# Attention blocks with two steps from scores to transposes, gate rows loaded per block, and the sixth token's first half moved ahead

## The chip, the cores and the metric

The kernel runs on one core of one Trainium2 chip. The metric is the device time of one execution in microseconds (us). The engines are PE (matrix multiplication, with PEld for its weight loads), DVE (vector), ACT (activations), POOL (GpSimd) and SP, which here only issues DMAs. Each engine runs its own instructions in order and waits on semaphores for the others.

## What is computed

One decoder block of 1024 positions of width 1024 in float32. After a norm and one projection, half of the width goes through a gated MLP (part A), half through forgetting attention with eight heads of 64 (part B). Both halves are normed, joined and projected; then follows a gated feed-forward network.

```python
n = rmsnorm(x);  proj = n @ w_in
a_out = spatial_gating(gelu(proj_u), gelu(proj_v), ...)          # part A
log_f = log_sigmoid(f_logit + b_f);  c = cumsum(log_f)           # part B
logits = (q_blk @ k_blk.T) * scale + c[q0:q1, None] - c[None, :q1]
p = softmax(where(mask, logits, -inf));  b_out = p @ v_blk
merged = concat(rmsnorm(a_out), rmsnorm(b_out));  mix = merged @ w_out
h = x + rmsnorm(mix);  out = h + rmsnorm(swiglu(rmsnorm(h)))
```

## The kernel before

Positions are cut into 8 token tiles of 128. Matrix products in float32 are made of three products of halves (`mm3`: high by high, high by low, low by high), so each operand is split on ACT (`L116`, high) and DVE (`L117`, low).

Attention takes the heads in four pairs. A pair has 8 units; a unit is one head `h` and one `m` of 0, 3, 1 or 2, and has two blocks, `i = 2m` and `2m + 1`: 128 queries against the `(i + 1) * 128` keys up to them. So there are 64 blocks, 16 in a pair, in the order 0, 1, 6, 7, 0, 1, 6, 7, 2, 3, 4, 5, 2, 3, 4, 5. Each block goes through four steps:
- `prep`: POOL adds the column `csq` to the gate row `cb` and writes the sum to the row tile `sm` (`L484`), then sets its masked part (`L486`). There are three `sm` tiles. `cb` holds the 1024 gate values of one head on all partitions. `cb_load` fetches it for the two heads of a pair.
- `scores`: PE makes the scores in one or two banks (`L502`) from the query piece `qu` and the keys; DVE adds the row and takes the least value (`L504`), ACT makes the exponential in `sm` (`L507`).
- `probs`: PE transposes the exponentials (`pt`, `L518`), ACT and DVE split them.
- `values` and `finish`, once per unit: PE multiplies with the values (`o`, `L547` to `L550`), ACT copies the result (`osb`, `L552`), PE transposes it back (`ot`, `L559`), ACT and DVE add its halves to `bt`, and for a pair of heads SP stores it to `bo_d`.

The loop over `n` runs the steps staggered: `prep` of block `n + 3`, `scores` of `n + 2`, `probs` of `n + 1`, and at every second `n` the values of a finished unit or the finish of the one before. Query pieces are loaded per unit in four DMAs (`qu_load`, `L471`). In the first three pairs `pump` fills the gaps with the projection matmuls of the next pair (`qk`), paced by the cost of the blocks. In the last pair the stages load the output weights (`load_wo`: `woraw`, eight loads of 512 KB over three stage buffers, split by ACT, DVE and POOL), and from step `SA` on `pump` fills with the output projection (`mx`) of tokens 0 and 1. `merge_a`, `merge_norm` and `merge_b` bring the two halves of a token to PE in transposed form (`tp_ma`, `tp_mb`); `mix_part` projects the four chunks `KA` of part A and the four `KB` of part B; `mix_tail` norms the result and adds x. `ORDER` lists the tokens: 0, 1, 6, 7, 2, 4, 3, 5. The text calls token 6, third in that list, the sixth token.

The order within an engine is not the program's: a scheduler places each instruction by its own estimate of when it can start, with the program's order as the priority. A DMA on SP also waits until the eighth DMA before it has landed, since eight semaphores take turns.

Of the kernel before, what the change touches and what calls it, by code (L numbers as in the profile page):

```python
# [7 lines left out]
F32 = mybir.dt.float32  # L8
# [23 lines left out]
LATE = 4  # L32
ORDER = [0, 1, 6, 7, 2, 4, 3, 5]
WB = 5
SMB = 3
QB = 2
QUB = 2
BTB = 3
# [2 lines left out]
FC = 2.0  # L41
WOS = (0, 1, 2, 3, 6, 7, 8, 9)
SA = 6
SB = 14
SLOPE = 90
LEAD = 10

# [2 lines left out]
def hybrid_block(ctx: ExitStack, tc: tile.TileContext, io: dict, out: bass.AP):  # L50
# [345 lines left out]

    at_cm = pool("att")
    at = at_cm.__enter__()
    qp, ks_, qus, cbs = {}, {}, {}, {}

    def qk_tile(tag, name, bufs):
        return at.tile([P, S], F32R, tag=tag, name=name, bufs=bufs)

    def cb_tile(name, dt=F32):
        return at.tile([P, S], dt, tag="cb", name=name, bufs=2)

    def osb_tile(name):
        return at.tile([P, 2 * P], F32, tag="osb", name=name, bufs=OSB)
# [9 lines left out]
    rrow = at.tile([P, S], F32, tag="rrow", name="rrow")  # L418
    nc.sync.dma_start(out=rrow.rearrange("p (t n) -> p t n", n=P),
                      in_=c_d[NH * NT:, :].rearrange("t n -> (t n)").partition_broadcast(P))  # L420
    cb0 = [cb_tile(f"cb_0_{h}") for h in range(2)]
    osb0 = osb_tile("osb_first")

    def cb_load(p):
        for h in range(2):
            c = cb_tile(f"cb_{p}_{h}") if p else cb0[h]
            g0 = (2 * p + h) * NT
            nc.sync.dma_start(out=c.rearrange("p (t n) -> p t n", n=P),
                              in_=c_d[g0:g0 + NT, :].rearrange("t n -> (t n)").partition_broadcast(P))
            cbs[2 * p + h] = c  # L430
# [42 lines left out]
    class Block:  # L473

        def __init__(self, unit, i):
            self.u, self.i = unit, i
            self.n = (i + 1) * P
            self.nm = f"{unit.hh}_{i}"

        def prep(self):  # L480

            i, n, hh = self.i, self.n, self.u.hh
            self.sm = sm = at.tile([P, S], F32, tag="sm", name=f"sm_{self.nm}", bufs=SMB)
            nc.gpsimd.tensor_scalar(out=sm[:, :n], in0=cbs[hh][:, :n], scalar1=csq[:, hh * NT + i:hh * NT + i + 1],  # L484
                                    scalar2=1.0, op0=ALU.add, op1=ALU.mult)
            nc.gpsimd.affine_select(out=sm[:, i * P:n], in_=sm[:, i * P:n], pattern=[[-1, P]], base=0,  # L486
                                    channel_multiplier=1, compare_op=ALU.is_ge, fill=BIG)
# [209 lines left out]
    qk_load(0, 1)  # L697
    for _ in qk_steps(0):
        pass
    cb_load(0)  # L700
    def qk_stream():
        for p in range(1, NPAIR):
            yield from qk_steps(p)
# [3 lines left out]
    def pump(upto):  # L707
        nonlocal done
        while done < upto:
            next(fill, None)  # L710
            done += 1
# [7 lines left out]
        x = (sum(cost[:m]) + part * cost[m]) / whole  # L719
        return min((NPAIR - 1) * QS, int(x * SLOPE + min(LEAD, 100 * x)))  # L720

    for n in range(-3, NB + 1):
        m = n + 2
        p, s = divmod(m, PB)
        if n + 3 < NB:
            if (n + 3) % PB == 0 and n + 3 > 0:
                cb_load((n + 3) // PB)
                pump((n + 3) // PB * QS)
            if (n + 3) % 2 == 0:
                qu_load(units[(n + 3) // 2])  # L730
            blocks[n + 3].prep()
        if 0 <= m < NB:
            if m == last:
                q0_cm.__exit__(None, None, None)
# [5 lines left out]
                nc.sync.dma_start(out=gb, in_=io["out_norm_b_gain"].partition_broadcast(P))  # L740
            blocks[m].scores()
        if last <= m:
            s = m - last
# [15 lines left out]
            if s == 9:  # L759
                for t in range(2):  # L760
                    nc.sync.dma_start(out=ab2[t], in_=bo_d[t * P:(t + 1) * P, :])
            if s in (11, 12):
                merge_norm(s - 11, ab2[s - 11], gb, junk)
            if s in (SB - 1, SB):
                merge_b(s - SB + 1, ab2[s - SB + 1])
            if s == SB:
                for _ in fill:
                    pass
                fill, done = mix_chain([(0, 0, KB, None), (0, 1, KB, None), (1, 0, KB, None)]), 0
            if s == 15:  # L770
                gains = [cb_tile(nm) for nm in ("gpm_att", "gpf_att")]
                load_gains(gains)
            if SA <= s < SB:
                pump((s - SA + 1) * 12 // (SB - SA))
            if s >= SB:
                pump((s - SB + 1) * 12 // (19 - SB))
        elif m >= 0:
            pump(pace(m, 0.5))
        if 0 <= n + 1 < NB:
            blocks[n + 1].probs()  # L780
        if 0 <= m < last:
            pump(pace(m, 1.0))
        if n >= 0 and n % 2 == 1:
            units[n // 2].values()
        if n >= 2 and n % 2 == 0:
            units[n // 2 - 1].finish(bts)
    for _ in fill:
        pass
    x_load(0)
# [36 lines left out]
    ab = {}  # L826

    def merge_start(t):
        a = ab[t] = flat(vs_tile(ORDER.index(t) % 2, f"ab_{t}"))
        rows = slice(t * P, (t + 1) * P)  # L830
        nc.sync.dma_start(out=a[:, :AW], in_=an_d[rows, :])
        nc.sync.dma_start(out=a[:, AW:], in_=bo_d[rows, :])
# [105 lines left out]
    order = ORDER  # L938
    merge_start(order[2])
    merge_start(order[3])  # L940
    for i, t in enumerate(order):
        if i == 7:
            raw_early(0, 1, 2)
        if i >= 2:
            for step, _ in enumerate(mix_chain([(t, 0, KALL, "mm"), (t, 1, KALL, "S")])):
                if i == 7 and step == 4:
                    pair_first(1)
                if i == 7 and step == 11:
                    norm2_first(3)
        if i in (3, 4, 6):  # L950
            j = {3: 0, 4: 1, 6: 2}[i]
            norm2_first(j)
            norm2_second(j)
        if i + 2 < NT:
            t2 = order[i + 2]
            merge_norm(t2, ab[t2][:, AW:], gb, junk)
        if i >= 2:
            mix_tail(t, gains, i == 7)
        if i + 2 < NT:
            x_load(t2)  # L960
            k = 2 + 2 * (i % 2)
            merged[t2] = (vs_tile(k, f"mh_{t2}"), vs_tile(k + 1, f"ml_{t2}"))
            merge_a(t2, ab[t2])
            merge_b(t2, ab[t2][:, AW:])
        if i + 4 < NT:
            merge_start(order[i + 4])
# [349 lines left out]
```

## Time and profile before

| | us |
|---|---|
| median of 3 runs (1131.88 to 1133.18) | 1132.99 |
| the profiled execution, whole | 1133.7 |
| its span, first to last instruction | 1132.0 |
| PE busy | 1095.6 |
| DVE busy | 719.4 |
| ACT busy | 527.9 |
| POOL busy | 162.6 |

The span is what the trace covers, and 1.7 us of the profiled execution lie outside of it. A busy PE is not PE at its peak, since matmuls overlap and their ends are modelled; what counts is how far apart their starts are. In a list of waits, "PE s L502 <- DVE st L504" means that PE stood before an instruction of line 502 and that the last event that it needed came from DVE's line 504. The granted clock is the share of PE's full 2.4 GHz.

### The profile page before, as it was taken

What the parts mean: (1) busy time and instruction counts of PE and PEld (TensorE: products, weight loads), DVE (VectorE), ACT (ScalarE), POOL (GpSimd) and SP (SyncE); (2) the same over time, 40 slices, a digit from 0 to 9 for tenths busy, and PEclk for the clock granted to TensorE, in tenths of its full rate; (3) what the DMA queues carried; (4) which work ended last, traced back from release to release, by engine and by line L of the source; (5) the groups of instructions that cost most, each with busy time, mean ns of one, the idle gap of its engine ahead of it and who ended that gap; (6) DMA issues with size and microseconds to landing.
All of it is one profiled execution on the core that took longest, in us unless ns stands there. A gap on an engine that the chain in (4) does not pass through costs nothing.

```text
span 1132.0 us, 15484 instructions
## 1 busy us (share of the span) xinstructions
PE 1095.6 (97%) x5353; PEld 910.2 (80%) x5353; DVE 719.4 (64%) x1225; ACT 527.9 (47%) x1017; POOL 162.6 (14%) x235
## 2 busy tenths in 40 slices
PE   6999999999999989999999999999999999999997
PEld 6988777888877768777888888888888888888885
DVE  6576325676668646789775667566756364644666
ACT  5444324666668534464433333333333345454552
POOL 3043113443337321000000000000000000000001
PEclk9999999999999999999999999999999999999999
DMA  7621013333255354457765564556455489766665
GB/s 263 213 93 33 34 74 105 86 88 103 75 156 166 118 191 139 158 182 227 260 225 186 189 217 163 204 177 237 154 191 185 145 287 321 224 191 195 192 201 169
DMA packets 87825, 192.99 MB, mean 170 GB/s; under 512 B 10236, under 2 KB 28740, under 8 KB 85060
## 3 DMA queue, kind: packets, MB, share of 16 engines
q1 hardware_dynamic: 87748, 192.01, 52.1%
q8 instruction: 42, 0.69, 0.3%
q14 instruction: 35, 0.29, 0.1%
HBM read 134.00 MB, written 49.58 MB: 162 GB/s over the span
## 4 chain that ended last, share of the span: by engine, by line
PE 81%; DVE 6%; DMA 4%; ACT 3%; issue 3%; POOL 2%; SPq 1%; POOLq 0%; DVEq 0%; ACTq 0%
PE guA L120 7%; PE guA L121 7%; PE guA L122 7%; PE guC L121 3%; PE guC L122 3%; PE guC L120 3%; PE dA L121 3%; PE dA L122 3%; PE dA L120 3%; PE dC L122 3%; PE dC L120 3%; PE dC L121 3%; PE qk L122 2%; PE qk L121 2%; PE qk L120 2%
## 5 line engine op out<-in xcount | busy, mean ns | idle before, releaser
L104 POOL TENSOR_TENSOR st<-st,mhalf 128x1 f32<-128x1 f32 x17 | 12.1, 715 | 663.4 <-DVE st L102 663.4
L117 DVE TENSOR_TENSOR dal<-dar,dah 128x512 fp32r<-128x512 f32 x77 | 53.2, 692 | 82.6 <-ACT dah L116 82.6
L116 ACT CAST dah<-dar 128x512 fp32r<-128x512 f32 x77 | 47.9, 622 | 97.9 <-PE dA L121 52.1
L117 DVE TENSOR_TENSOR ptl<-pt,pth 128x512 fp32r<-128x512 f32 (+2 forms) x96 | 51.6, 554 | 27.8 <-ACT pth L116 27.1
L121 PE MATMUL dA<-dwl,dah 128*128 128x512 f32 x176 | 68.7, 390 | 0.2 <-DVE dwl L117 0.2
L120 PE MATMUL dA<-dwh,dah 128*128 128x512 f32 x176 | 68.5, 389 | 0.0
L122 PE MATMUL dA<-dwh,dal 128*128 128x512 f32 x176 | 68.5, 389 | 0.0
L484 POOL TENSOR_SCALAR sm<-cb,csq 128x128 f32<-128x128 f32 (+3 forms) x64 | 50.8, 794 | 98.2 <-PE pt L518 75.1
L507 ACT ACTIVATE sm<-sm,st 128x128 f32<-128x128 f32 (+3 forms) x64 | 49.9, 780 | 17.4 <-DVE st L504 16.6
L116 ACT CAST pth<-pt 128x512 fp32r<-128x512 f32 (+2 forms) x96 | 43.6, 476 | 26.2 <-PE pt L518 25.8
L117 DVE TENSOR_TENSOR dwl<-dwr,dwh 128x512 fp32r<-128x512 f32 x77 | 52.7, 685 | 2.3 <-ACT dwh L116 2.3
L117 DVE TENSOR_TENSOR fbc_0l<-ts,fbc_0h 128x1024 fp32r<-128x1024 f32 x22 | 26.9, 1224 | 42.1 <-ACT fbc_0h L116 42.1
L502 PE MATMUL s<-k,qu 128*128 128x384 f32 (+4 forms) x192 | 51.1, 368 | 2.6 <-DVE st L504 2.4
L120 PE MATMUL qk<-nth,qkw 128*128 128x512 f32 x128 | 53.4, 418 | 0.0
L120 PE MATMUL mx<-woh,mh 128*128 128x512 f32 x128 | 52.2, 408 | 1.2 <-ACT mh L116 1.1
L122 PE MATMUL mx<-woh,ml 128*128 128x512 f32 x128 | 50.9, 400 | 1.2 <-DVE ml L117 1.2
L120 PE MATMUL dC<-dwh,dah 128*128 128x512 f32 x132 | 51.3, 389 | 0.0
L121 PE MATMUL dC<-dwl,dah 128*128 128x512 f32 x132 | 51.3, 389 | 0.0
L122 PE MATMUL dC<-dwh,dal 128*128 128x512 f32 x132 | 51.3, 389 | 0.0
L121 PE MATMUL mx<-wol,mh 128*128 128x512 f32 x128 | 51.2, 400 | 0.0
L121 PE MATMUL qk<-ntl,qkw 128*128 128x512 f32 x128 | 50.7, 396 | 0.0
L122 PE MATMUL qk<-nth,qkw 128*128 128x512 f32 x128 | 50.5, 395 | 0.1
(749 smaller groups left out, 3243.4 us busy)
## 6 DMA issues: line engine op xcount, KB each, us to landing
graw<-in_w_gu SPq DMA_DIRECT2D x21, 1024.0 KB, 5.4
wj<-in_w_ffn_out SPq DMA_DIRECT2D x22, 512.0 KB, 4.1
aj<-ff_d SPq DMA_DIRECT2D x22, 512.0 KB, 4.3
dar<-as_d SPq DMA_DIRECT2D x44, 256.0 KB, 3.8
dwr<-ws_d SPq DMA_DIRECT2D x44, 256.0 KB, 3.9
dwr<-in_w_ffn_out SPq DMA_DIRECT2D x33, 256.0 KB, 4.2
dar<-ff_d SPq DMA_DIRECT2D x33, 256.0 KB, 4.3
ff_d<-g SPq DMA_DIRECT2D x22, 256.0 KB, 5.4
```

The source lines that it names most:

```text
L104: nc.gpsimd.tensor_tensor(out=r, in0=m, in1=mhalf, op=ALU.pow)
L116: nc.scalar.copy(out=hi, in_=src)
L117: (lo_eng or nc.vector).tensor_tensor(out=lo, in0=src, in1=hi.bitcast(F32), op=ALU.subtract)
L120: nc.tensor.matmul(o, ah, bh, start=first, stop=False, **kw)
L121: nc.tensor.matmul(o, ah, bl, start=False, stop=False, **kw)
L122: nc.tensor.matmul(o, al, bh, start=False, stop=last, **kw)
L484: nc.gpsimd.tensor_scalar(out=sm[:, :n], in0=cbs[hh][:, :n], scalar1=csq[:, hh * NT + i:hh * NT + i + 1], scalar2=1.0, op0=ALU.add, op1=AL ...
L502: nc.tensor.matmul(o[:, :w], qu[:, hl, ts], ks_[hh][:, ks], start=hl == 0, stop=hl == 1)
L507: nc.scalar.activation(sm[:, :n], sm[:, :n], AF.Exp, bias=m, scale=-1.0, accum_out=rsum[:, self.i, hh:hh + 1])
```

## The change

The row tiles `sm` become five, and `cb` goes. Each block now has a step `load` that fetches its own part of the gate row by a broadcast DMA right into `sm`; `prep` adds to it in place. The loop is staggered by one step more between scores and transposes: `load` of `n + 5`, `prep` of `n + 4`, `scores` of `n + 3`, `probs` of `n + 1`. `finish` comes before `values` at odd `n`, two iterations behind the values of its unit. The steps that prepare tokens 0 and 1 move back by two (`SB` and the constants 9 to 12). Token 6 gets its part A loaded into a row tile and transposed within the loop, its `KA` product directly behind token 1's tail, and the third turn of the later loop is written out there.

```diff
-SMB = 3
+SMB = 5
...
-SB = 14
+SB = 16
...
+        def load(self):
+
+            self.sm = sm_tile(f"sm_{self.nm}")
+            g0 = self.u.hh * NT
+            nc.sync.dma_start(out=self.sm[:, :self.n].rearrange("p (t n) -> p t n", n=P),
+                              in_=c_d[g0:g0 + self.i + 1, :].rearrange("t n -> (t n)").partition_broadcast(P))
...
-            nc.gpsimd.tensor_scalar(out=sm[:, :n], in0=cbs[hh][:, :n], scalar1=csq[:, hh * NT + i:hh * NT + i + 1],
+            nc.gpsimd.tensor_scalar(out=sm[:, :n], in0=sm[:, :n], scalar1=csq[:, hh * NT + i:hh * NT + i + 1],
...
-    for n in range(-3, NB + 1):
-        m = n + 2
...
+    blocks[0].load()
+    for n in range(-4, NB + 2):
+        m = n + 3
+        s = m - last
+        if n + 5 < NB:
+            blocks[n + 5].load()
+        if n + 4 < NB:
+            if (n + 4) % PB == 0:
+                pump((n + 4) // PB * QS)
+            if n % 2 == 0:
+                qu_load(units[n // 2 + 2])
+            blocks[n + 4].prep()
...
+            if s == 16:
+                t2 = ORDER[2]
+                a = sm_tile(f"a_{t2}")[:, :AW]
+                nc.sync.dma_start(out=a, in_=an_d[t2 * P:(t2 + 1) * P, :])
+                merged[t2] = [qk_tile(f"q{x}", f"m{x}_{t2}", 2).rearrange("p (k t) -> p k t", t=P) for x in "hl"]
+                merge_a(t2, a)
...
-                pump((s - SB + 1) * 12 // (19 - SB))
+                pump((s - SB + 1) * 12 // (21 - SB))
...
-        if n >= 0 and n % 2 == 1:
-            units[n // 2].values()
-        if n >= 2 and n % 2 == 0:
-            units[n // 2 - 1].finish(bts)
+        if n % 2 == 1:
+            if n >= 3:
+                units[n // 2 - 1].finish(bts)
+            if 0 < n < NB:
+                units[n // 2].values()
...
+    t = ORDER[2]
+    merge_start(t, (1,))
+    merge_start(ORDER[3])
+    merge_b_norm(2)
+    merge(2)
+    for _ in mix_chain([(t, 0, KA, "mm"), (t, 1, KA, "S")]):
+        pass
+    merge_b_norm(3)
+    merge(3)
+    for _ in mix_chain([(t, 0, KB, None), (t, 1, KB, None)]):
+        pass
```

What this does to the order of the instructions shows at three places. The first is ACT in the last head pair, from the exponential of block 6 of head 6 to the first copy of that block's transposes (`sm_6_6` is head 6, block 6; `pth` the high half of its transposes). Before:

```order
L507 ACTIVATE sm_6_6_3867,rsum_66<-sm_6_6_3867,st1_148_3920 128x896
L116 CAST mh_0_3839<-tp_ma0_0_3931 128x512
L116 CAST pth_6_0_0_3888<-pt_6_1_0_3938 128x2x128
L566 COPY bt_2_2_3752<-ot_5_2_3943 128x2x64
L116 CAST woh3_3972<-woraw3_3970 128x512
L586 CAST woh3_3972<-woraw3_3970 128x512
L116 CAST mh_1_3841<-tp_ma1_0_3978 128x512
L116 CAST pth_6_3_0_3990<-pt_6_6_0_3985 128x4x128
```

The same place on ACT after:

```order
L504 ACTIVATE sm_6_6_3809,rsum_66<-sm_6_6_3809,st1_148_3931 128x896
L549 COPY osb_5_2_3974<-o_5_2_3961 128x256
L116 CAST woh2_3936<-woraw2_3934 128x512
L583 CAST woh2_3936<-woraw2_3934 128x512
L504 ACTIVATE sm_6_7_3880,rsum_66<-sm_6_7_3880,st1_150_3995 128x1024
L116 CAST mh_1_3845<-tp_ma1_0_4006 128x512
L116 CAST pth_6_0_0_3951<-pt_6_1_0_4013 128x2x128
L116 CAST pth_6_3_0_4035<-pt_6_6_0_4030 128x4x128
```

The exponential of the next block, `sm_6_7`, now stands between the two.

The second place is SP's queue in the last pair, around the query pieces of head 7's unit 3 (`qu_7_3`). Before:

```order
L581 DMA woraw3_3970<-in_w_out 128x1024
L581 DMA woraw4_4097<-in_w_out 128x1024
L471 DMA qu_7_3_4040<-qh_3_3007 64x256 x2
L471 DMA qu_7_3_4040<-ql_3_3008 64x256
L570 DMA bo_d_69<-bt_2_2_3752 128x2x128
```

SP at the same place after:

```order
L578 DMA woraw3_3998<-in_w_out 128x1024
L475 DMA sm_7_6_4018<-c_d_70 128x896
L462 DMA qu_7_3_4062<-qh_3_3018 64x256
L475 DMA sm_7_7_4060<-c_d_70 128x1024
L462 DMA qu_7_3_4062<-qh_3_3018 64x256
L462 DMA qu_7_3_4062<-ql_3_3019 64x256
L567 DMA bo_d_69<-bt_2_2_3866 128x2x128
```

The row loads of blocks 6 and 7 of head 7 now stand among the query pieces, each waiting for PE's transposes of the block five places before.

The third place is PE where token 1 ends (`mx_1_1`) and token 6 begins. Before:

```order
L120 MATMUL mx_1_1_4642<-woh7_4239,mh_1_3841 128x512
L121 MATMUL mx_1_1_4642<-wol7_4240,mh_1_3841 128x512
L122 MATMUL mx_1_1_4642<-woh7_4239,ml_1_1_3843 128x512
L129 MATMUL tp_ma6_0_4739<-ident_63,ab_6_4720 128x128 x4
L120 MATMUL mx_6_0_4786<-woh0_3830,mh_6_4737 128x512
L121 MATMUL mx_6_0_4786<-wol0_3831,mh_6_4737 128x512
```

PE at the same place after:

```order
L120 MATMUL mx_1_1_4701<-woh7_4261,mh_1_3845 128x512
L121 MATMUL mx_1_1_4701<-wol7_4262,mh_1_3845 128x512
L122 MATMUL mx_1_1_4701<-woh7_4261,ml_1_1_3847 128x512
L120 MATMUL mx_6_0_4773<-woh0_3834,mh_6_4564 128x512
L121 MATMUL mx_6_0_4773<-wol0_3835,mh_6_4564 128x512
```

The transposes `tp_ma6` have gone ahead into the loop, and token 6's product follows token 1's at once; it is followed by `tp_mb6` as before.

## Rows read from the trace of the kernel before

**Rows 1.** The page: busy time and share of the span, by engine.
```profile
PE 1095.6 (97%) x5353; PEld 910.2 (80%) x5353; DVE 719.4 (64%) x1225; ACT 527.9 (47%) x1017; POOL 162.6 (14%) x235
```
**Rows 2.** Windows: stretch, length, busy by engine; last the clock, DMA share, GB/s.
```profile
187.00:331.00 144.00, 141.73 (x865) 121.41 (x866) 97.48 (x259) 91.79 (x236) 57.30 (x100) 1.00 0.33 86
331.00:345.00 14.00, 11.69 (x70) 9.69 (x69) 13.12 (x33) 12.23 (x30) 6.16 (x9) 0.88 0.72 236
345.00:384.00 39.00, 33.57 (x212) 27.09 (x212) 28.21 (x74) 28.25 (x71) 25.79 (x36) 1.00 0.55 168
384.00:403.30 19.30, 19.30 (x108) 16.21 (x107) 10.71 (x27) 8.97 (x23) 3.19 (x4) 1.00 0.37 124
403.30:407.30 4.00, 1.94 (x10) 1.18 (x9) 2.42 (x5) 1.16 (x3) 0.55 (x1) 1.00 0.35 127
407.30:411.30 4.00, 4.00 (x11) 3.14 (x12) 2.12 (x3) 2.48 (x6) 0.55 (x1) 0.57 0.57 181
```
**Rows 3.** Waits of PE, 331 to 403 us: us in total, times, longest.
```profile
PE s L502 <- DVE st L504: 2.0, 4, 1.1
PE ot L559 <- DVE ptl L117: 1.7, 2, 1.4
PE ot L559 <- ACT osb L552: 1.4, 2, 0.8
PE pt L518 <- DVE ptl L117: 0.9, 2, 0.6
...
PE pt L518 <- ACT sm L507: 0.4, 1, 0.4
```
**Rows 4.** Instructions on the row tiles and loads, least/median/most ns.
```profile
L484 POOL TENSOR_SCALAR sm<-cb,csq x64: 366/798/1442, 172.5 to 381.9; 128x128 f32<-128x128 f32 x8, 128x256 f32<-128x256 f32 x8, 128x896 f32<-128x896 f32 x8, 128x1024 f32<-128x1024 f32 x8
L428 SPq DMA_DIRECT2D cb<-c_d x8: 326/490/533, 165.8 to 330.6; - x8
...
L486 POOL TENSOR_SCALAR_AFFINE_SELECT sm<-sm x64: 285/293/760, 173.3 to 383.0; 128x128 f32<-128x128 f32 x64
```
**Rows 5.** DMA issues, 187 to 331 us: count, KB each, median us to landing.
```profile
cb<-c_d SPq DMA_DIRECT2D x6, 512.0 KB, 3.7
qu<-ql SPq DMA_DIRECT2D x46, 64.0 KB, 2.0
```
**Rows 6.** DMA issues, 331 to 384 us.
```profile
qu<-ql SPq DMA_DIRECT2D x14, 64.0 KB, 3.5
...
ab<-an_d SPq DMA_DIRECT2D x2, 256.0 KB, 4.7
...
gpm_att<-in_post_mix_gain SPq DMA_DIRECT2D x1, 512.0 KB, 5.3
```
**Rows 7.** Waits of SP's queue, 331 to 384 us.
```profile
SPq L581 <- POOL wol L587: 3.6, 1, 3.6
```
**Rows 8.** Timeline 403 to 414 us: start, us, instruction, count, idle before.
```profile
403.30 0.60 PE L129 MATMUL tp_ma<-ident,ab 128*128 128x128 f32 x4
403.49 0.60 ACT L656 ACTIVATE tmp<-mx 128x512 f32<-128x512 f32 x1 [3.84 <-PE mx L122]
...
404.71 0.50 PE L120 MATMUL mx<-woh,mh 128*128 128x512 f32 x1 [0.82 <-ACT mh L116]
...
406.42 0.68 DVE L117 TENSOR_TENSOR ml<-tp_ma,mh 128x512 fp32r<-128x512 f32 x1
...
407.15 0.54 PE L122 MATMUL mx<-woh,ml 128*128 128x512 f32 x1 [1.24 <-DVE ml L117]
407.49 0.63 PE L120 MATMUL mx<-woh,mh 128*128 128x512 f32 x1
...
411.36 0.39 PE L120 MATMUL mx<-woh,mh 128*128 128x512 f32 x1
...
412.27 0.75 DVE L612 SCALAR_TENSOR_TENSOR ab<-ab,st,gb 128x512 f32<-128x512 f32 x1 [0.66 <-POOL st L111]
...
413.43 0.60 PE L129 MATMUL tp_mb<-ident,ab 128*128 128x128 f32 x4
```

More of the change, by code (lines that the diff above doesn't have):

```diff
@@ L398, in hybrid_block, with sm_tile @@
     at = at_cm.__enter__()
-    qp, ks_, qus, cbs = {}, {}, {}, {}
+    qp, ks_, qus = {}, {}, {}
     def qk_tile(tag, name, bufs):
         return at.tile([P, S], F32R, tag=tag, name=name, bufs=bufs)
-    def cb_tile(name, dt=F32):
-        return at.tile([P, S], dt, tag="cb", name=name, bufs=2)
+    def sm_tile(name):
+        return at.tile([P, S], F32, tag="sm", name=name, bufs=SMB)
     def osb_tile(name):
@@ L420, in hybrid_block @@
                       in_=c_d[NH * NT:, :].rearrange("t n -> (t n)").partition_broadcast(P))
-    cb0 = [cb_tile(f"cb_0_{h}") for h in range(2)]
     osb0 = osb_tile("osb_first")
[L424 to L430, printed above, removed]
     def qk_steps(p):
@@ L478, in __init__ @@
             self.nm = f"{unit.hh}_{i}"
+        def load(self):
[3 more added lines that the diff above has]
+                              in_=c_d[g0:g0 + self.i + 1, :].rearrange("t n -> (t n)").partition_broadcast(P))
         def prep(self):
-            i, n, hh = self.i, self.n, self.u.hh
-            self.sm = sm = at.tile([P, S], F32, tag="sm", name=f"sm_{self.nm}", bufs=SMB)
-            nc.gpsimd.tensor_scalar(out=sm[:, :n], in0=cbs[hh][:, :n], scalar1=csq[:, hh * NT + i:hh * NT + i + 1],
+            i, n, hh, sm = self.i, self.n, self.u.hh, self.sm
+            nc.gpsimd.tensor_scalar(out=sm[:, :n], in0=sm[:, :n], scalar1=csq[:, hh * NT + i:hh * NT + i + 1],
                                     scalar2=1.0, op0=ALU.add, op1=ALU.mult)
@@ L699, in hybrid_block @@
         pass
-    cb_load(0)
     def qk_stream():
@@ L720, in pace @@
         return min((NPAIR - 1) * QS, int(x * SLOPE + min(LEAD, 100 * x)))
-    for n in range(-3, NB + 1):
-        m = n + 2
[L724 to L731, printed above, removed]
+    blocks[0].load()
[10 more added lines that the diff above has]
+            blocks[n + 4].prep()
         if 0 <= m < NB:
@@ L742, in hybrid_block @@
         if last <= m:
-            s = m - last
             if s in WOS:
@@ L758, in hybrid_block @@
                 fill, done = mix_chain([(0, 0, KA, "mm"), (0, 1, KA, "mm"), (1, 0, KA, "X")]), 0
-            if s == 9:
+            if s == 11:
                 for t in range(2):
                     nc.sync.dma_start(out=ab2[t], in_=bo_d[t * P:(t + 1) * P, :])
-            if s in (11, 12):
-                merge_norm(s - 11, ab2[s - 11], gb, junk)
+            if s in (13, 14):
+                merge_norm(s - 13, ab2[s - 13], gb, junk)
             if s in (SB - 1, SB):
@@ L770, in hybrid_block @@
             if s == 15:
-                gains = [cb_tile(nm) for nm in ("gpm_att", "gpf_att")]
+                gains = [sm_tile(nm) for nm in ("gpm_att", "gpf_att")]
                 load_gains(gains)
+            if s == 16:
[4 more added lines that the diff above has]
+                merge_a(t2, a)
             if SA <= s < SB:
@@ L794, in hybrid_block, with merge_start, merge_b_norm, merge @@
     mix_tail(1, gains)
+    ab = {}
+    def merge_start(t, halves=(0, 1)):
+        a = ab[t] = flat(vs_tile(ORDER.index(t) % 2, f"ab_{t}"))
+        rows = slice(t * P, (t + 1) * P)
+        for h in halves:
+            nc.sync.dma_start(out=a[:, h * AW:(h + 1) * AW], in_=(an_d, bo_d)[h][rows, :])
+    def merge_b_norm(i):
+        merge_norm(ORDER[i], ab[ORDER[i]][:, AW:], gb, junk)
+    def merge(i):
+        t = ORDER[i]
+        x_load(t)
+        if t not in merged:
+            k = 2 + 2 * (i % 2)
+            merged[t] = (vs_tile(k, f"mh_{t}"), vs_tile(k + 1, f"ml_{t}"))
+            merge_a(t, ab[t])
+        merge_b(t, ab[t][:, AW:])
+        if i + 2 < NT:
+            merge_start(ORDER[i + 2])
+    t = ORDER[2]
[9 more added lines that the diff above has]
+        pass
+    merge_b_norm(4)
+    mix_tail(t, gains)
+    merge(4)
     at_cm.__exit__(None, None, None)
@@ L824, in s_tile @@
         return pl.tile([P, 512], F32, tag="s", name=name, bufs=n)
[L826 to L832, printed above, removed]
     def kview(t):
@@ L936, in product @@
                 skip_group_check=not first)
[L938 to L941, printed above, removed]
+    for i in range(3, NT):
+        t = ORDER[i]
         if i == 7:
             raw_early(0, 1, 2)
[L944 to L949, printed above, removed]
+        for step, _ in enumerate(mix_chain([(t, 0, KALL, "mm"), (t, 1, KALL, "S")])):
+            if i == 7 and step == 4:
+                pair_first(1)
+            if i == 7 and step == 11:
+                norm2_first(3)
         if i in (3, 4, 6):
@@ L954, in hybrid_block @@
         if i + 2 < NT:
[L955 to L958, printed above, removed]
+            merge_b_norm(i + 2)
+        mix_tail(t, gains, i == 7)
         if i + 2 < NT:
[L960 to L966, printed above, removed]
+            merge(i + 2)
         if i in (4, 5):
```

## The prediction

> **What bounds the kernel now.** I read the page's busy shares first. PE is busy for 1095.6 us of a span of 1132.0 us [rows 1], so at most 36 us can be won by filling its idle time. Next I cut the stretch that the change touches into stages [rows 2]. The scores and values of the first three head pairs run from 187 to 331 us; there PE is idle for only 144.00 - 141.73 = 2.3 us, while DVE and ACT have a third of their time free. The projection matmuls (`qk`) that are mixed in fill the gaps. The last head pair runs from 331 to 384 us without that filler: PE is idle for 14.00 - 11.69 = 2.3 and 39.00 - 33.57 = 5.4 us, 7.7 us in 53 us. From 384 to 403.3 us the output projection fills PE completely. Then 2.1 us of 4.0 are idle, and the next 4 us show a granted clock of 0.57, which is mostly the lower level of 1.2 GHz. So the change can win in two places: the last head pair, and the few us from 403.3 on.
>
> Who ends PE's idle time in the last pair [rows 3]? Scores wait 2.0 us for a score bank that DVE has not read yet; the transposes of the output block (`ot`) wait 1.7 us for DVE and 1.4 us for ACT's copy of the values; transposes of the exponentials wait 0.9 us for a bank, and only 0.4 us for the exponential itself. The reader should see that the wait which the new distance removes by its meaning, transposes for ACT's `sm`, is the smallest of them.
>
> **The distance of two steps.** Before, a block is scored one step before it is transposed; after, two. ACT's order shows that it does happen: one more exponential stands between a block's exponential and the copies of its transposes. The output's transposes also move, from one step behind the values to two. No instruction is added on PE. Directly, rows 3 give 0.4 us (exponential) and 1.4 us (ACT's copy before `ot`). The waits on DVE (2.0 + 1.7 + 0.9 us) are partly a matter of capacity: from 331 to 345 us DVE is busy for 13.12 of 14.00 us, and no distance helps there; from 345 to 384 us it is busy for 28.21 of 39.00 us [rows 2], so there the waits come from order, and slack does help. I take half of those 4.6 us, 2.3 us. That makes 0.4 + 1.4 + 2.3 = 4.1 us. The ceiling is all idle time of the stretch, 7.7 us, and with the low clock of 331 to 345 us (0.88, some 1.5 us of work at 1.2 GHz) 9 us.
>
> **Gate rows by DMA.** Before, POOL adds a column to a row tile (`cb`) that is loaded once per head, 8 loads of 512 KB. After, each block loads its own piece into `sm` and POOL works in place. The work of POOL is the same 64 + 64 instructions of about 0.8 and 0.3 us [rows 4]. The loads grow from 8 to 64: per head (1 + 2 + ... + 8) x 64 KB = 2.36 MB, 18.9 MB in all instead of 4.2. 56 more issues at about 0.5 us [rows 4] are 28 us of SP's queue in 200 us, and SP can spare that. What matters is what stands behind them. Each row load waits until PE has transposed the block five places before. Behind it on SP stand the query pieces (`qu`), the loads of the output weights (`woraw`) and the stores of finished blocks; PE waits for `qu`, ACT and POOL for `woraw`. From that transposition to the scores five places on lie 2.5 steps. In the first three pairs a step is 144 us / 48 = 3.0 us, so 7.5 us; around the short blocks it is about 5.2 us, counted from PE's order at 0.23 us per 512 columns. The chain is: issue 0.5 us, a 512 KB row 3.7 us [rows 5], POOL 1.4 + 0.3 us for the longest row, 5.9 us in all, and a `qu` piece issued behind it 0.5 + 2.0 us. Scores need only `qu`; the row is needed by DVE's reduction after them. So PE stays covered there; I take a gain of 1.0 us out of the 2.3 us, with bounds of -2.3 and +1.5 us. In the last pair a step is 53 / 16 = 3.3 us and the 2.5 steps are 8.3 us, but there the queues are fuller: `qu` needs 3.5 us to land where it needed 2.0, and the other loads up to 5.3 us [rows 5, 6], and SP stood for 3.6 us behind a weight load that waited for POOL [rows 7]. My term is a loss of 0.6 us: two such late pieces of 0.3 us. The bounds are 0 (8.3 us cover 5.9) and 7.5 us (the second rival).
>
> Rows 5 and 6 show that the same 64 KB piece lands after 2.0 us where the DMA engines are busy for 0.33 of the time and after 3.5 us where they are at 0.55 to 0.72 [rows 2]. The Trainium skill's page DMA: Bandwidth & Descriptors, section Queues, rings and completion order, says that on each DMA engine descriptors are consumed in ring order. By that rule a small load does not pass a row load issued before it; the trace agrees in direction. By the rule every piece behind a 512 KB row would land with it, 3.7 us instead of 2.0, 1.7 us later; by the rows it mostly has those 1.7 us to spare.
>
> A second effect: POOL's wait for a free row tile moves to SP. I count nothing for it, since POOL is idle for two fifths of the last pair anyhow (6.16 + 25.79 of 53 us busy [rows 2]).
>
> **The drain.** The loop runs two iterations longer, with the same work on PE; the output projection is spread over it. The first half of the sixth token (`a`, 256 KB) is loaded into a row tile that comes free when block 61 is transposed, behind two gains and an x row of 512 KB each. Its transposes stand some 2.9 us of PE work behind that block (ten matmuls of 0.23 us, as the nine from 411.36 to 413.43 us stand apart [rows 8], and five shorter instructions). A 256 KB load lands after 4.7 us [rows 6]. So PE waits between 0 and 1.7 us; I take 0.7 us.
>
> **The sixth token's half early.** Before [rows 8]: PE ends token 1 at 403.30 us, transposes the sixth token's first half, waits 0.82 us for ACT and 1.24 us for DVE, and runs 24 matmuls, of which the ten from 407.49 to 411.36 us take 3.87 us instead of 2.33; at 413.43 us it reaches the transposes of the second half. But DVE ends that second half's norm only at 413.02 us, because its chain (ACT square, DVE, POOL, again ACT) stands behind token 1's tail, which starts at 403.49 us. After: the 24 matmuls (5.6 us) follow token 1 at once, the 0.6 us of DVE `ml` leave the chain, and the rest of the chain stays: 9.7 - 0.6 = 9.1 us after token 1. PE saves 10.1 - 9.1 = 1.0 us and now stands still for 3.5 us in one piece. The last time that 2.06 us of idle time in 4 us came, the clock fell to its lower level, which cost those 3.87 - 2.33 = 1.5 us, hidden then under the chain; now it would lie behind it, on the path. So this part gives between -1.0 and +0.5 us; I take -0.2 us. From 414 us on the order is the same, and so I count nothing there.
>
> **The sum.** -4.1 (distance) - 1.0 (first three pairs) + 0.6 (late pieces) + 0.7 (drain) - 0.2 (sixth token) = -4.0 us against the profiled execution's 1133.7 us: 1129.7 us. That execution lies 0.7 us above the median of the runs, so I forecast 1129.0 us.
>
> **The rivals.**
> - *The distance is worth little.* The last pair is set by DVE and ACT, busy for 0.78 and 0.76 of it, and by in-order queues that stop on weight loads. Then only 0.4 + 1.4 us go, the drain gives back 0.7 us, and the sixth token's half gives nothing: 1133.0 - 1.1 = 1131.9 us. For it speaks that DVE is full from 331 to 345 us; against it, that half of the idle time comes later. Chance 0.24.
> - *Slower: SP's queue in the last pair.* A weight load waits for POOL to free its stage, a row load for PE, and the rest of the query pieces stand behind both (the rows of SP in the change's section). Five of the eight weight loads need a freed stage. If each holds the queue long enough that PE waits 1.5 us for `qu` (8.3 us of cover less 3.6 us of waiting for POOL, 0.5 us of issue, 0.5 us and up to 5.3 us of landing gives -1.6 us), that is +7.5 us; with half of the other gains left the time is 1133.0 + 7.5 - 2.5 = 1138.0 us. It decides from about 0.8 us per wait. For it speaks that `qu` lands late there already; against it, that two steps of slack absorb what delays DVE and ACT. Chance 0.18.
> - *The idle time in the tail, on the path.* The clock falls (+0.5 us), `a` is late (+1.7 us), the first three pairs lose 1.5 us and the distance gives only 0.4 us: 1133.0 + 3.3 = 1136.3 us. Chance 0.08.
>
> That the change does not do what it says is excluded by the order of the instructions.
>
> **How the numbers follow.** The forecast, faster by more than 0.2% (2.3 us, about what a measurement of this kernel can tell from no change, so below 1130.7 us), holds 0.50, with its own range of 1124 to 1130.7 us. Within 0.2% holds 0.24 (the first rival), slower 0.26 (the two others). To leave out no more than 2 in 10, the range goes from 1129.0 - (9 - 4.1) = 1124 us (the last pair's ceiling reached) to 1138 us (the second rival): 1124 to 1138.
>
> **What would show it.** Right: in the last pair PE's idle time falls from 7.7 us to about 4, the waits of `ot` on ACT vanish, no scores wait for a DMA, and PE has one gap of about 3.5 us before the sixth token's second half. Wrong: PE waits for `qu` in the last pair, its clock falls after the tail's gap, or the first three pairs get longer than 144 us. What would upset it most is a last pair that DVE holds at its old length.

## The result, and the profile after

The changed kernel takes 1144.76 us (median of 4 runs, 1144.34 to 1145.16), the kernel before 1132.8 us beside it: a ratio of 1.0105, 95% interval 1.0093 to 1.0117, so 12 us slower. The forecast was 1129.0 us with a range up to 1138. The profiled execution has a span of 1143.3 us against 1132.0.

Where the 11.3 us of span come from can be read off PE's progress: add up PE's matmuls in order (0.233 us per 512 columns, 0.1 us per transpose) and ask when each kernel has done the same sum. The changed kernel's lag behind the one before, at the times of the one before:

| time in the kernel before, us | 187 | 320 | 344 | 376 | 380 | 400 | 440 | 1120 |
|---|---|---|---|---|---|---|---|---|
| lag, us | -0.7 | -0.6 | 3.1 | 3.5 | 9.1 | 10.2 | 11.5 | 11.4 |

Nothing is lost in the first three pairs and nothing after 440 us. The last pair costs 3.7 us at its entry, 5.6 us at one place and 1.1 us in the drain, the sixth token's tail 1.3 us. The same in the windows (answers to [rows 2]: stretch, length, busy time of PE, PEld, DVE, ACT, POOL, clock, DMA share, GB/s):

```profile
187.00:331.00 144.00, 141.63 (x864) 121.98 (x863) 96.20 (x254) 91.09 (x234) 54.51 (x96) 1.00 0.55 157
...
337.80:348.20 10.40, 8.63 (x38) 7.68 (x36) 7.09 (x18) 6.15 (x18) 5.81 (x8) 0.51 0.76 214
348.20:381.00 32.80, 29.71 (x178) 23.62 (x177) 23.08 (x60) 23.98 (x58) 18.72 (x25) 1.00 0.73 218
381.00:385.70 4.70, 1.11 (x7) 0.62 (x6) 1.34 (x8) 1.91 (x6) 3.15 (x5) 0.99 0.97 322
385.70:392.50 6.80, 5.25 (x22) 4.86 (x23) 4.23 (x11) 2.40 (x9) 2.01 (x3) 0.50 0.39 133
392.50:413.70 21.20, 21.05 (x117) 17.26 (x117) 10.99 (x24) 10.61 (x26) 3.41 (x5) 1.00 0.37 122
413.70:423.20 9.50, 5.79 (x25) 4.31 (x23) 5.94 (x9) 3.17 (x8) 1.93 (x4) 1.00 0.41 146
423.20:426.70 3.50, 3.09 (x11) 2.68 (x12) 2.32 (x5) 1.17 (x2) 0.55 (x1) 0.51 0.66 208
```

PE runs at 1.2 GHz (0.50) for about 10.2, 6.8 and 3.4 us, each time after a stretch with idle time; before, the 0.88 of 14 us and the 0.57 of 4 us [rows 2] make 3.4 us twice. The 3.7 us at the pair's entry are for the most part this: 10.2 us at half the clock in place of 3.4 us cost up to 3.4 us, while no wait there is over 1.1 us. PE's waits from 331 to 414 us, the answer to [rows 3]:

```profile
PE o L544 <- ACT pth L116: 5.3, 3, 4.1
PE pt L515 <- DVE ptl L117: 2.4, 4, 1.1
PE s L499 <- DMA qu<-qh: 2.0, 2, 1.4
PE s L499 <- DVE st L501: 0.9, 1, 0.9
PE pt L515 <- ACT sm L504: 0.9, 1, 0.9
```

The waits of `ot` for ACT (1.4 us) and half of those of scores for DVE (2.0 to 0.9) are gone, as forecast; transposes of the exponentials wait longer than before, for DVE (0.9 to 2.4) and for the exponential (0.4 to 0.9). Two new kinds come on top: scores wait for query pieces, and the values (`o`) wait for ACT's copies, 4.1 us at once. That one wait is the 5.6 us at 380 us, with the low clock behind it. Its chain, from the timeline (start, us, instruction; in brackets the idle time before and who ended it):

```profile
378.78 0.88 SPq L758 DMA_DIRECT2D ab<-bo_d  x2
...
381.37 1.16 PE L515 MATMUL pt<-ident,sm 128*128 128x128 f32 x6 [0.33 <-DVE ptl L117]
...
382.46 0.80 POOL L481 TENSOR_SCALAR sm<-sm,csq 128x640 f32<-128x640 f32 x1 [3.01 <-PE pt L515]
...
383.59 2.04 POOL L605 TENSOR_TENSOR ab<-ab,rsum 128x512 f32<-128x512 f32 x2
...
384.67 0.63 ACT L607 ACTIVATE junk<-ab 128x512 bf16<-128x512 f32 x1 [2.72 <-POOL ab L605]
...
386.00 0.83 ACT L116 CAST pth<-pt 128x512 fp32r<-128x512 f32 x2
...
386.62 0.58 PE L544 MATMUL o<-pth,vs 128*128 128x256 f32 x1 [4.09 <-ACT pth L116]
```

PE has transposed block 59 by 382.53 us, and ACT could copy it. But ACT issues in order, and token 0's square (`L607`) stands before the copy. It waits for POOL's product of `ab`, which waits for the load of `ab` (issued at 378.8 us, before at 370.7) and stands behind the `prep` of block 62, whose row has only just landed. In the kernel before, the square also stood before the copies of that block. But ACT waited 1.48 us for it, PE had four matmuls of `mx` to do meanwhile, and then stood for 1.35 us:

```profile
376.81 0.63 ACT L610 ACTIVATE junk<-ab 128x512 bf16<-128x512 f32 x1 [1.48 <-POOL ab L608]
...
378.78 0.44 PE L559 MATMUL ot<-ident,osb 128*128 128x128 f32 x2 [1.35 <-DVE ptl L117]
```

So it is not the place of the square that is new, but how late what it waits for comes. ACT's order after, from the exponential of block 60 on (`pt_6_5` is block 59):

```order
L504 ACTIVATE sm_7_2_4284,rsum_66<-sm_7_2_4284,st1_163_4384 128x384
L607 ACTIVATE junk_3824,st1_165_4441<-ab_3840 128x512
L504 ACTIVATE sm_7_3_4341,rsum_66<-sm_7_3_4341,st1_164_4436 128x512
L116 CAST pth_6_2_0_4395<-pt_6_5_0_4452 128x4x128
L116 CAST pth_6_2_1_4401<-pt_6_5_4_4459 128x2x128
```

### The profile page after: what moved, and what is told of

The parts are those of the page before. It is cut to its first block, busy times and chain, and to the rows that moved or that the text cites. A ratio compares the mean times of both kernels' runs of the same rounds, so it can differ in the third digit from the quotient of the medians.

```text
span 1143.3 us, 15592 instructions
## 1 busy us (share of the span) xinstructions
PE 1098.8 (96%) x5353; PEld 913.3 (80%) x5353; DVE 719.4 (63%) x1225; ACT 527.9 (46%) x1017; POOL 161.9 (14%) x235
## 4 chain that ended last, share of the span: by engine, by line
PE 56%; DVE 4%; DMA 1%; issue 1%; POOL 1%; ACT 0%; POOLq 0%; DVEq 0%; SPq 0%; ACTq 0%
PE guA L120 6%; PE guA L122 6%; PE guA L121 6%; PE dA L121 3%; PE dA L122 3%; PE guC L122 3%; PE dA L120 3%; PE guC L121 3%; PE guC L120 3%; PE dC L122 3%; PE dC L120 3%; PE dC L121 3%; PE guE L121 2%; PE guE L122 2%; PE guE L120 2%; PE mx L120 1%
## 5 line engine op out<-in xcount | busy, mean ns | idle before, releaser
L481 POOL TENSOR_SCALAR sm<-sm,csq 128x128 f32<-128x128 f32 (+3 forms) x64 | 49.8, 779 | 102.7 <-DMA sm<-c_d 56.4
```

The lines of the kernel that those rows point to most:

```text
L481: nc.gpsimd.tensor_scalar(out=sm[:, :n], in0=sm[:, :n], scalar1=csq[:, hh * NT + i:hh * NT + i + 1], scalar2=1.0, op0=ALU.add, op1=ALU.mult)
```

## The experiments

Theory Q: the row loads are the cause, through queues, order or bytes. Its rivals: D, the distance itself; F, the order in which PE's filler is used; T, the sixth token's half. All times stand beside runs of the kernel before on the same chip. "Pair" and "tail" are how much the lag of the profiled execution grows from 320 to 400 us and from 400 to 440 us of the kernel before; they come from one execution each, and that of e5, e7 and e15 is 3 to 5 us over its median, so a few us of them are chance.

| run | median us (lowest to highest) | ratio to before, 95% interval | pair | tail |
|---|---|---|---|---|
| after | 1144.8 (1144.3 to 1145.2) | 1.0105 (1.0093 to 1.0117) | +10.8 | +1.3 |
| e1_no_rows | 1134.2 (1132.3 to 1136.8) | 1.0008 (0.9997 to 1.0019) | -1.8 | +1.6 |
| e2_rows_only | 1139.5 (1137.9 to 1140.5) | 1.0050 (1.0035 to 1.0065) | +7.1 | -1.0 |
| e3_sixth_late | 1146.9 (1143.8 to 1147.6) | 1.0112 (1.0095 to 1.0128) | +11.5 | +0.8 |
| e4_short_rows | 1138.7 (1136.5 to 1138.9) | 1.0045 (1.0029 to 1.0062) | -0.1 | +2.1 |
| e5_two_cb | 1135.1 (1131.6 to 1138.5) | 1.0015 (1.0000 to 1.0031) | 0.0 | +2.3 |
| e6_two_cb_late | 1133.1 (1130.8 to 1137.0) | 1.0006 (0.9991 to 1.0020) | -2.7 | 0.0 |
| e7_filler_kept | 1146.3 (1144.1 to 1151.7) | 1.0121 (1.0094 to 1.0148) | +13.2 | +1.6 |
| e8_rows_on_act | 1153.4 (1152.0 to 1157.3) | 1.0178 (1.0157 to 1.0199) | +14.8 | +0.9 |
| e10_norm_later | 1143.9 (1142.9 to 1146.5) | 1.0092 (1.0076 to 1.0108) | +6.8 | +2.7 |
| e11_no_weights | 1136.6 (1136.1 to 1139.1) | 1.0033 (1.0019 to 1.0047) | +1.3 | +0.7 |
| e12_more_tiles | 1142.6 (1140.4 to 1144.4) | 1.0080 (1.0063 to 1.0096) | +5.0 | +1.0 |
| e13_qu_ahead | 1142.5 (1141.4 to 1144.9) | 1.0083 (1.0068 to 1.0098) | +7.1 | +1.3 |
| e14_tiles_norm | 1136.5 (1135.8 to 1137.6) | 1.0038 (1.0024 to 1.0053) | +1.2 | +1.9 |
| e15_tiles_norm_late | 1135.6 (1131.4 to 1139.4) | 1.0027 (1.0009 to 1.0045) | +4.4 | +1.1 |

**e1_no_rows**, against the changed kernel:

```diff
-            nc.sync.dma_start(out=self.sm[:, :self.n].rearrange("p (t n) -> p t n", n=P),
-                              in_=c_d[g0:g0 + self.i + 1, :].rearrange("t n -> (t n)").partition_broadcast(P))
...
-            nc.gpsimd.tensor_scalar(out=sm[:, :n], in0=sm[:, :n], scalar1=csq[:, hh * NT + i:hh * NT + i + 1],
+            nc.gpsimd.tensor_scalar(out=sm[:, :n], in0=rrow[:, :n], scalar1=csq[:, hh * NT + i:hh * NT + i + 1],
```

> The changed kernel without its 64 row loads: prep adds the column to a tile that is resident anyhow (rrow), so POOL's work, the distance of two steps and the sixth token's early half stay; the scores get the wrong gate row. Theory Q (the row loads on SP's queue are the cause: query pieces and the tokens' loads land behind them, PE stops and its clock falls): 1130 to 1134 us, the last head pair back to about 53 us. Theory D (the distance is the cause: the norms of tokens 0 and 1 now stand before the transposes' copies on POOL and ACT and hold PE 4.1 us): still 1140 us or more, with PE's wait of 4 us for pth in it.

0.2 us above Q's range, far from D's: without the row loads 11 us are back (1.0105 to 1.0008), and the pair is 1.8 us shorter than before. The gap at 382 us is gone; the distance alone does no harm that shows. Leaving the loads out has also moved ACT's square behind the copies of block 59 (375.69 us against 373.27), so this run does not tell the loads from the order that comes with them.

**e2_rows_only**, against the kernel before (one step, four `sm` tiles):

```diff
+        if n + 4 < NB:
+            blocks[n + 4].load()
         if n + 3 < NB:
```

> The kernel before with the row loads alone: four row tiles, the load of n + 4 one iteration ahead of its prep as in the changed kernel, distance of one step, sixth token as before. Theory Q: 1140 to 1144 us, PE waiting for qu in the last pair. Theory D: 1132 to 1135 us, since the order of the norms against the transposes is that of before.

Just under Q's range: the loads alone cost 6 us at the old distance too. PE's waits from 330 to 440 us show the same two kinds as after:

```profile
PE o L545 <- ACT pth L116: 2.3, 1, 2.3
PE s L500 <- DMA qu<-qh: 2.1, 2, 1.5
```

**e3_sixth_late**: the block at `s == 16` is left out, and the tail goes back to the old order.

```diff
-            if s == 16:
...
-                merge_a(t2, a)
...
-    merge_start(t, (1,))
+    merge_start(t)
```

> The changed kernel with the sixth token's first half back behind token 1. If the gap of 4.1 us and the low clock after it cost on the path, 1143.5 us, 1.2 us less than the changed kernel's 1144.8; if the half early is worth the 0.2 us that the prediction gave it, 1145.0 us.

Above both figures: 1.0112 against 1.0105, intervals overlapping. Undoing the half wins nothing that shows, and having it neither; what it costs stays below what this pair can tell.

**e4_short_rows**, against the changed kernel:

```diff
-            nc.sync.dma_start(out=self.sm[:, :self.n].rearrange("p (t n) -> p t n", n=P),
-                              in_=c_d[g0:g0 + self.i + 1, :].rearrange("t n -> (t n)").partition_broadcast(P))
+            nc.sync.dma_start(out=self.sm[:, :P], in_=c_d[g0:g0 + 1, :].rearrange("t n -> (t n)").partition_broadcast(P))
```

> The changed kernel with 64 row loads of 64 KB each (the first 128 columns; prep reads the resident tile and writes over them, so that it still waits for the load): the number of issues and SP's waits for PE stay, the bytes fall from 18.9 to 4.2 MB. Theory Q by bytes (a query piece lands behind a long row): 1131 to 1135 us. Theory Q by queue (SP stands before a row load until PE frees the tile, and the pieces behind it are issued late): 1141 us or more. Theory D: 1140 us or more.

Between the cases: 6.1 us less than after by the medians, 5.2 more than before; in the trace the pair loses nothing. I took this for a vote for the bytes. It is none, because the shorter loads also changed the order: in ACT's row the square now stands behind the copies of block 59. e14 decides it.

**e5_two_cb** and **e6_two_cb_late** (with and without the early sixth half): distance of two steps with gate rows per head.

```diff
-        return at.tile([P, S], F32, tag="sm", name=name, bufs=SMB)
+        return at.tile([P, w], F32, tag=f"sm{w}", name=name, bufs=2)
...
+            self.sm = sm_tile(f"sm_{self.nm}", 512 if self.i < 4 else S)
...
+                if n > -4:
+                    cb_load((n + 4) // PB)
```

> The changed kernel's distance of two steps and its early sixth half, but the gate rows loaded once per head into cb as before; row tiles of two sizes (two of 1024 columns for blocks 4 to 7, two of 512 for blocks 0 to 3) keep four blocks in flight in the space of the kernel before. Nothing is left out. Theory Q (the row loads are the cause): as the run without rows, 1133 to 1135 us. Rival (four tiles are one too few, POOL waits for PE): 1137 us or more.

> As the run with gate rows once per head, with the sixth token's first half behind token 1 again. The progress of the run without rows over the kernel before: the distance won 1.8 us in the last pair and the tail lost 1.6 us after it. If the early half is what the tail lost, 1131.5 to 1132.5 us, just faster than before; if the tail's loss comes from the later drain, 1133.5 us or more.

e5 came 0.1 us above Q's range (1135.1), e6 0.4 us under the second case of its forecast. e6 is the distance by itself, with the longer loop and in the old memory: 1.0006 (0.9991 to 1.0020). It is worth nothing that can be measured, at most 1 us. The early half lies between the two, 2 us of medians with overlapping intervals.

**e8_rows_on_act**:

```diff
-            nc.sync.dma_start(out=self.sm[:, :self.n].rearrange("p (t n) -> p t n", n=P),
+            nc.scalar.dma_start(out=self.sm[:, :self.n].rearrange("p (t n) -> p t n", n=P),
```

> The changed kernel with the same 64 row loads of 18.9 MB issued by ACT instead of SP. If the loss comes from SP's queue (a query piece is issued behind a row load that waits for PE, or stands in the same ring behind it): 1134 to 1138 us. If it comes from the bytes on the DMA engines, whoever issues them: 1140 to 1145 us. If ACT, which issues in order, stands before a row load until PE frees its tile: over 1146 us.

The time is that of the third case. The loads stand among ACT's copies and are issued later still; POOL waits 18.5 us for rows (331 to 400 us; in the changed kernel 10.4 us up to 405), and DVE and PE behind it:

```profile
POOL sm L481 <- DMA sm<-c_d: 18.5, 9, 4.2
```

So this run does not part SP's ring from the bytes.

**e10_norm_later**:

```diff
-            if s in (13, 14):
-                merge_norm(s - 13, ab2[s - 13], gb, junk)
+            if s in (14, 15):
+                merge_norm(s - 14, ab2[s - 14], gb, junk)
...
-            if s in (SB - 1, SB):
-                merge_b(s - SB + 1, ab2[s - SB + 1])
+            if s in (SB, SB + 1):
+                merge_b(s - SB, ab2[s - SB])
```

> The changed kernel with the norms of tokens 0 and 1 and what follows from them one step later (14, 15 and 16, 17 instead of 13, 14 and 15, 16). PE's order up to the gap at 382 us stays; ACT's square no longer stands before the copy of block 59's transposes. If the gap is ACT's queue behind a late load: the wait of 4.1 us goes to about 0.7, the low clock of 6.8 us behind it goes, 1138.5 to 1140 us. If PE is bound by the row loads there anyhow: 1143 us or more.

The gap went as expected: `o` waits for ACT 1.2 us in all instead of 5.3, PE keeps its clock there, the pair loses 6.8 us instead of 10.8. But the time is that of the other case, 1143.9 us. The tail gave part of it back: token 6's gap grew from 4.1 to 4.8 us, and the low clock behind it from 3.4 to 6.8 us:

```profile
PE tp_mb L129 <- DVE st L109: 4.8, 1, 4.8
PE s L499 <- DMA qu<-qh: 3.6, 4, 1.7
```

**e7_filler_kept**:

```diff
-            if s in (2, 3):
-                merge_a(s - 2, ab2[s - 2])
+            if s in (2, 10):
+                merge_a(int(s == 10), ab2[int(s == 10)])
```

> The changed kernel with token 1's first half transposed eight steps later (step 10 instead of 3), so that the 12 last matmuls of the output projection that fill the pair cannot be used up before step 10: in PE's order they stand between 370 and 382 us of the changed kernel, where its trace has none. Theory F (the row loads make the scheduler expect late scores and fill PE with the projection early, and the late waits then lie bare): the idle time from 370 to 387 us is filled, 1139 to 1142 us. If the waits are set by loads and queues whatever fills PE: 1143 to 1146 us.

F falls in this form: 1146.3 us, and `o` still waits 3.6 us for ACT (in the trace of the slowest run, 1151.7 us), with `mx` right ahead of the gap. Filler before the gap does not shorten a chain that runs over SP, POOL and ACT. Filler inside the gap, as in the kernel before, was not tested; its four `mx` were 0.9 us of work.

**e11_no_weights**:

```diff
-        raw = stage(f"woraw{k}")[:, :D]
-        nc.sync.dma_start(out=raw, in_=io["w_out"][k * P:(k + 1) * P, :])
+        raw = rrow
```

> The changed kernel with the eight loads of the output weights left out (4.2 MB of the last pair; their splitting reads a resident tile), row loads as they are (4.7 MB in the pair). Theory Q by bytes (row and weight loads together are too much for the last pair): 1133 to 1137 us. If the row loads alone hold the pair, by SP's order or by their landing: 1141 us or more.

1136.6 us, Q by bytes as it seemed; but SP also has eight issues less, and the square stands behind block 59's copies here too.

**e12_more_tiles** and **e13_qu_ahead**:

```diff
-        return at.tile([P, S], F32, tag="sm", name=name, bufs=SMB)
+        return at.tile([P, w], F32, tag=f"sm{w}", name=name, bufs=3 if w == S else 4)
...
+            self.sm = sm_tile(f"sm_{self.nm}", 512 if self.i < 4 else S)
```

e13 has three tiles of each size and, besides:

```diff
-QUB = 2
+QUB = 3
...
-                qu_load(units[n // 2 + 2])
+                for u in units[n // 2 + 3:n // 2 + 4] if n > -4 else units[:2]:
+                    qu_load(u)
```

> The changed kernel with the same 20 KB of row tiles cut into three of 1024 columns (blocks 4 to 7) and four of 512 (blocks 0 to 3): a tile comes free five to eight blocks earlier than it is loaded again instead of five, so SP stands less before a row load; bytes and issues are the same. Theory Q by queue (SP waits for PE with query pieces behind the row load): 1136 to 1140 us. Theory Q by bytes: 1142 to 1146 us.

> The changed kernel with row tiles of two sizes (three of each, 18 KB) and in the 2 KB that this saves a third query tile: each unit's query pieces are issued one unit earlier. If the query pieces that land behind rows are what starts the loss (PE waits 2.2 us for them in the last pair, and its clock falls): no wait of PE for qu, 1138 to 1141 us. If the rows themselves and the loads of the tokens come too late: 1143 us or more.

Both 2 to 3 us better than after by ratio: e12 meets the case of the bytes, e13 lies between its two, and one wait for `qu` of 1.4 us stays in it. But in e12 the waits for `qu` are gone from PE's list, and at 376 us the kernel is 1.5 us ahead of the one before; then the gap comes all the same. SP's waits for PE before a row load, 331 to 384 us, first of the changed kernel, then of e12:

```profile
SPq L475 <- PE pt L515: 14.6, 7, 4.7
```

```profile
SPq L475 <- PE pt L515: 3.9, 2, 3.5
```

**e14_tiles_norm** is e12 and e10 together, **e15_tiles_norm_late** that with the sixth half late.

> Both repairs together: row tiles of two sizes (three and four, SP stands less before a row load) and the norms of tokens 0 and 1 one step later (ACT's square behind the copy of block 59's transposes); all 64 row loads, all bytes, the early sixth half stay. The first repair alone left the gap of 4 us at 381 us, the second alone left the waits for query pieces. If queue and order are the whole price of the row loads in the last pair: no gap over 2 us in it, 1135.5 to 1138 us (the tail's loss stays). If the bytes cost by themselves: 1139.5 us or more.

> As the run with both repairs, and the sixth token's first half back behind token 1. The tail gives back 1.3 to 2.5 us if the early half is its loss: 1133.5 to 1136 us; the same as the run with both repairs if the later norms are.

e14 keeps every byte and every issue, and takes 1136.5 us: 8 of the 12 us are back. Against e12 the later norms are worth 4.8 us by ratio, against e10 the tiles are worth 6.1 us, and the intervals lie apart. Alone they gave 1.5 and 2.8 us; that both give more than this sum is not shown, since the 3.3 us between are no more than the error of the four ratios. The traces part the two repairs. At the entry (320 to 344 us) the lag grows by 3.7 us in the changed kernel and by 3 in e10, but by 0.4 or less in e12 and e14. From 376 to 380 us it grows by some 5.5 us in the changed kernel and e12, but by 0.6 or less in e10 and e14. PE's waits in e14 from 331 to 400 us, and the window of the pair before, after and in e14:

```profile
PE s L499 <- DMA qu<-qh: 2.2, 2, 1.3
PE pt L515 <- ACT sm L504: 2.1, 2, 1.4
...
PE o L544 <- ACT pth L116: 0.3, 1, 0.3
```

```profile
331.00:384.00 53.00, 45.26 (x280) 36.78 (x279) 41.34 (x106) 40.47 (x100) 31.95 (x44) 0.97 0.59 186
331.00:384.00 53.00, 44.14 (x250) 35.58 (x248) 37.97 (x98) 36.85 (x90) 28.41 (x39) 0.90 0.76 228
331.00:384.00 53.00, 45.95 (x279) 36.85 (x277) 40.05 (x109) 40.62 (x100) 29.52 (x39) 0.97 0.82 251
```

The DMA engines are busier than in the changed kernel (0.82 against 0.76 in the same 53 us), and the pair loses 1.2 us instead of 10.8. So most of it was queue and order, not bytes. Tiles that come free earlier let the rows land earlier, and also what stands behind them on SP; no run parts these two. e15, 1135.6 us with a wide spread, lies in its first case but can't be told from e14; its profiled execution was the slowest of its seven. No version beat the kernel before; e6 equals it.

## Why the prediction was wrong

**What bounds the kernel** was read rightly: the change acts in the last pair and the tail, and nowhere else.

**The distance**: forecast -4.1 us, measured +0.7 us, with an interval that leaves at most 1 us of gain (e6). In single traces the pair is 1.8 and 2.7 us shorter (e1, e6) or as long as before (e5), but the time does not show it. The waits for ACT that were to go, 1.4 and 0.4 us, did go in e6. The term that was mis-sized is the half of the 4.6 us of DVE waits: in e6 3.5 us of them are left, not 2.3, and values wait 0.6 us for ACT's copies besides:

```profile
PE s L509 <- DVE st L511: 1.5, 3, 0.8
PE ot L566 <- DVE ptl L117: 1.1, 2, 0.9
PE pt L525 <- DVE ptl L117: 0.9, 1, 0.9
PE o L554 <- ACT pth L116: 0.6, 2, 0.4
```

The first rival, which gave the distance 1.8 us, was nearer.

**The gate rows** are the step that decided. First three pairs: forecast -1.0 us (-2.3 to +1.5), measured +0.1, although a 512 KB row landed after 5.3 us and not 3.7; the cover held. Last pair: forecast +0.6 us with bounds 0 to 7.5, measured some 11 us (after against e1, by ratio, the whole kernel), beyond the bound. The step that failed is that 8.3 us of cover hold the 5.9 us of a row's chain, and that POOL's wait costs nothing on SP. Three parts of its working failed.
- The cover of 8.3 us was counted from the moment a tile comes free, with SP ready to issue. SP stood 14.6 us before row loads (rows above), and what stands behind them started late. I had counted nothing for moving POOL's wait to SP, since POOL is idle anyhow; but SP's queue also carries the query pieces and the tokens' loads. In the kernel before, POOL stood 9.0 us for those transposes and held only its own work; SP held every load behind it, and POOL still waits for rows (331 to 405 us):

```profile
POOL sm L481 <- DMA sm<-c_d: 10.4, 5, 2.3
```

  The loss at the entry, low clock and all, goes with it: in the traces of e12 to e15, with more row tiles and all bytes, the entry loses 0.4 us or less (SP stands 3.9 us before row loads in e12). It also goes where bytes are left out (e4, e11).
- The landing times were taken from single rows. In the changed kernel, loads issued from 358.3 to 361.3 us:

```profile
woraw<-in_w_out SPq DMA_DIRECT2D x1, 512.0 KB, 5.7
sm<-c_d SPq DMA_DIRECT2D x1, 256.0 KB, 6.3
qu<-qh SPq DMA_DIRECT2D x2, 64.0 KB, 6.0
qu<-ql SPq DMA_DIRECT2D x2, 64.0 KB, 5.4
```

A 64 KB piece took 5.2 to 6.0 us behind a weight and a row, not 3.5 [rows 6], and PE waited 1.35 us for it at 365 us. It is these few that cost: over the whole pair the median rose from 3.2 to 4.4 us for `qh` and fell from 3.5 to 3.1 us for `ql`. The row and the three pieces behind it, issued from 358.4 to 360.6 us, landed at 364.7, 365.3, 365.6 and 365.8 us: the pieces come with what was issued before them, and all 196 DMAs of SP from 187 to 430 us whose landing the trace shows landed in the order of issue. The Trainium skill (DMA: Bandwidth & Descriptors, section Queues, rings and completion order) says that on each DMA engine descriptors are consumed in ring order; the trace agrees. It is the rule that I weighed and set aside.
- The largest piece, 5.6 us, was not in the sum at all: token 0's square before the copy of block 59 in ACT's order. The square stood before that copy in the old order and in the new one, of which the prediction read only the place around the exponentials; it did not ask when the square's input would come. That the loads bring the gap is shown by e2 (it comes with them at the old distance, 2.3 us), that it is ACT's order by e10, and that it and SP's queue together are most of the loss by e14. The remaining 3.4 us between e14 and e1 (1.0038 against 1.0008) were not settled; e14 still waits 2.2 us for `qu`, and the bytes may have a part in that.

The second rival named SP's queue in the last pair, but behind weight loads, and priced it at 7.5 us; it was the nearest, 6.8 us too low. At 0.18 it had too little, and the range ended with it.

**The drain**: forecast +0.7 us for `a`. No wait for `a` shows in the changed kernel (e10 has one of 0.8 us). What the drain lost, 1.1 us, follows the gap.

**The sixth token's half**: forecast -0.2 us (-1.0 to +0.5), in the trace +1.3 us. Token 1 ends at 413.74 us, and the rest of the timeline reads:

```profile
413.74 0.39 PE L120 MATMUL mx<-woh,mh 128*128 128x512 f32 x1
...
423.61 1.12 PE L129 MATMUL tp_mb<-ident,ab 128*128 128x128 f32 x4 [4.12 <-DVE st L109]
424.52 1.06 PE L129 MATMUL tp_ma<-ident,ab 128*128 128x128 f32 x4
```

From token 1's end to the second half are 9.9 us, not 9.1 (10.1 before): 0.3 us won instead of 1.0. The 0.6 us of `ml` left the chain as forecast, but DVE took up token 1's sum of squares 1.48 us after its end and not 0.92: the last product of token 0 (`L677`, 1.28 us) stood before it. The clock fell behind the gap of 4.1 us, on the path: the second half starts 10.2 us later than in the kernel before (423.61 against 413.43 us), and by 440 us the lag is 11.5 us. These 1.3 us are nearly the 1.5 us that I had put as the clock's whole price. In the timed pairs (e5 and e6, after and e3, e14 and e15) the part's sign stays open.

**What would show it**: the waits of `ot` on ACT vanished and the gap before token 6's second half came (4.1 us against 3.5), as written. PE's idle time in 331 to 384 us did not halve, it rose from 7.7 us to 53.00 - 44.14 = 8.9 us. Of the three signs of an error, scores that wait for `qu` and the clock after the tail's gap both appeared.

## What to carry to other kernels

When a change moves a wait from an engine to the queue that issues its loads, list everything that is issued behind it: a wait on an engine with idle time holds only that engine, the same wait on a shared queue holds every consumer. When a scheduler places the instructions, read the whole order of each in-order engine for an instruction that stands before the bound engine's next input while waiting for a chain of loads, and ask how late that chain now ends. Loads left out or shortened also changed that order here (e1, e4, e11), though no arithmetic on ACT was touched, so such runs do not tell bytes from order. And mend such faults together before judging one of them: here each repair alone gave under 3 us, both gave 8.

## What the runs showed of the hardware

The same gap did not bring the same clock: after 4.1 us of waiting at 382 us the granted clock was 0.50 for 6.8 us, after 4.1 us in the tail 0.51 for 3.4 us, and at the pair's entry it was 0.50 for 10.2 us with no wait over 0.9 us ahead of it. And in single traces the pair lost 10.8 us with a DMA share of 0.76 at 228 GB/s (the changed kernel) and 1.2 us with 0.82 at 251 GB/s (e14): how full the DMA engines are did not tell who waits. Whether the bytes cost anything by themselves stays open.
